# The output projection's first two tiles emitted inside attention, and head 7's first half ordered ahead of head 6's second half

## The chip, the cores and the metric

The kernel runs on one core of one Trainium2 chip. The metric is the device time of one execution in microseconds, as the median of several runs. Less is better. The engines are TensorE (PE; its weight loads are listed apart as PEld), VectorE (DVE), ScalarE (ACT), GpSimd (POOL) and SyncE (SP), which here issues the transfers.

## The reference

The kernel computes two layers of a decoder trunk over 1024 tokens of width 1024 in float32. Each layer normalises x, makes one wide input projection and feeds three branches: a causal convolution (256 channels), latent attention with 8 heads, and a spatial gating unit (256 channels). Each branch output is gated and RMS-normalised; the three are concatenated, go through one output projection and are added to x.

```python
for l in range(DEPTH):                       # 2
    h = _rms_norm(x, norm_g[l]); proj = h @ w_in[l]
    y_conv = _conv_branch(a, a_glu, ...) * silu(z_conv)
    y_mla  = _mla_branch(c_q, c_kv, k_rope, ...) * silu(z_mla)   # 8 heads, causal, 96 wide q/k, 64 wide v
    y_sg   = _sgu_branch(u_sg, v_sg, ...) * silu(z_sg)
    y = concatenate([rms(y_conv), rms(y_mla), rms(y_sg)])        # 256 + 512 + 256
    x = x + y @ w_out[l]
```

## The kernel before, in words

Tokens are cut into 8 tiles of 128. Every large product is made from operands split into a high and a low fp32r part, with three matmuls per product (`mm3`, L157): hi by hi, hi by lo, lo by hi. ScalarE casts the high part, VectorE subtracts it for the low part (`split`, L167 to L170). PSUM is given out as four single banks (`bank`, tag b1) and two double ones (`bank2`, tag b2). Scores, and the transposes of a whole token tile (`chan_of`, written pt or pty), use the double ones.

The order of the work is written out in two steps. `Flow` and, in attention, a planner hold estimated times and decide in which order instructions are emitted. The tile framework then fixes each engine's queue from that list by a clock of its own, so that work which is ready can pass work that isn't; on the chip each engine keeps that order. Memory is given out in pools that are opened and closed like a stack on two sides; a tile that takes over memory waits for whoever used it last.

Attention (`attention`, L982) keeps three lists: `sq` (transposes of q and k, scores with their softmax, weight splits and early loads), `tq` (transposes of probabilities for a head, a half of 512 queries and a key tile j) and `pq` (products with v, and `finish`, which transposes a pair of heads' sums, `ot`, and multiplies them into zsm). It takes the entry that can start first by its estimates. Half 0 has 4 key tiles, half 1 has 8. `tq` goes through the heads in order, half 0 before half 1. The scores of head h's half are emitted only after the previous head's last transpose of the same half, and the wide probabilities have four buffers (tag p1). The even heads' q and k lie in pool T1, the odd heads' in pool T. After head 7's half 0 is finished, tiles 0 and 1 of the attention output are normed (`early_norm`, L862): ScalarE squares, VectorE and GpSimd scale.

After attention pool T is closed and pool Ya opened in its place. For tiles 0 and 1 the branch outputs are transposed into yT (`chan_of`, written pty), which is a tile of Ya; the other tiles follow with two tiles' lead. `y_out` (L899) makes the projection of one token tile and one half of the output columns with 24 matmuls into the tile po, and `y_add` (L915) adds x and stores the result. The halves are c = 0 and 1, each over all 8 tiles. Loads of the side branches (`y_load`, tile yn) and of x (`x_load`, tile xr or xt) go through SP's queue. In the first layer the pass c = 1 also norms the next layer's input (`s0_next`, L954).

```python
        for i in (0, 1):                                      # L934
            sd, ym = early_src.pop(i)
            chan_of([...], y_tile(i, yp_), 0, f"pty{l}_{i}")
            y_load(i + 2); y_norm(i + 2); x_load(0, i)
    tq = []                                                   # L1136
    for h in range(H):
        for half in (0, 1):
            tq += [(h, half, j) for j in range(4 * half + 4)]
```

Of the kernel before, what the change touches and what calls it, by code (L numbers as in the profile page):

```python
# [126 lines left out]
def hybrid_trunk(ctx, tc, x, w, pc, pr, sgw, pww, cst, out):  # L127
# [235 lines left out]
    for l in range(L):  # L363
# [56 lines left out]
        def layer_norm_stats(srcs, mv, rstd):  # L420
# [5 lines left out]
            rsqrt(rstd, rstd)  # L426

        def v_done(p, o):
            vg = ap_.tile([P, 2, SW], F32, tag="e2k", bufs=5 - l, name=f"vg{l}_{p}")
            nc.scalar.activation(vg, pair(o), AF.Gelu_apprx_tanh)  # L430

            def rest():
                mv = ap_.tile([P, 2, 2], F32, tag="mv", bufs=4, name="mv")
                rstd = ap_.tile([P, 2], F32, tag="rstd", bufs=4, name="rstd")
                layer_norm_stats([vg[:, 0, :], vg[:, 1, :]], mv, rstd)
                for t in (0, 1):
                    nc.vector.tensor_scalar(vg[:, t, :], vg[:, t, :], mv[:, t, 0:1],
                                            rstd[:, t:t + 1], op0=ALU.subtract, op1=ALU.mult)
                flow.at(VN_LAG[l], gains)

            def gains():
                nc.gpsimd.tensor_tensor(out=vg, in0=vg, in1=bc_mid(slg, 2), op=ALU.mult)
                nc.gpsimd.tensor_tensor(out=vg, in0=vg, in1=bc_mid(slb, 2), op=ALU.add)
                if p % 2 == 0:
                    vn.append(sp.tile([P, NT // 2, SW], F32R, tag="h", bufs=5 - l, name=f"vl{l}_{p}"))
                hi, lo = vn[0][:, 2 * p:2 * p + 2, :], vn[-1][:, p % 2 * 2:p % 2 * 2 + 2, :]
                nc.scalar.copy(hi, vg)
                nc.gpsimd.tensor_tensor(out=lo, in0=vg, in1=hi.bitcast(F32), op=ALU.subtract)
            flow.at(0.8, rest)
# [78 lines left out]

        sgs = sp.tile([P, 2, SH, P], F32R, tag="h", bufs=5 - l, name=f"sgs{l}")
        nc.scalar.copy(sgs[:, 0], sgm)  # L530
# [79 lines left out]
        def conv_swish(p, nt):  # L610
            b = bank(f"cb{l}_{p}")
            for ct in (0, 1):
                for t in (0, 1):
                    tr(b[:, ct * 256 + t * P:ct * 256 + (t + 1) * P], nt[:, t, ct * P:(ct + 1) * P])
            sT = ap_.tile([P, 2, 256], F32, tag="sT", bufs=1, name="sT")
            th = ap_.tile([P, 2, 256], F32, tag="th", bufs=1, name="th")
            for ct in (0, 1):
                src = b[:, ct * 256:(ct + 1) * 256]
                nc.scalar.activation(th[:, ct, :], src, AF.Tanh, scale=dpc[:, 62 + ct:63 + ct],
                                     bias=dpc[:, 64 + ct:65 + ct])  # L620
                nc.scalar.activation(sT[:, ct, :], src, AF.Identity,
                                     scale=pcs[:, PC_LG + ct:PC_LG + ct + 1],
                                     bias=pcs[:, PC_LB + ct:PC_LB + ct + 1])
            nc.vector.scalar_tensor_tensor(out=sT, in0=th, scalar=1.0, in1=sT,
                                           op0=ALU.add, op1=ALU.mult)
            if not pws:
                pws.append(parts_of(pwt, "pws", nc.gpsimd))
            ss = parts_of(sT, f"ss{p}", nc.vector)
            flow.at(4.0, lambda: conv_point(p, ss))
# [3 lines left out]
        def parts_of(a, name, eng):  # L633
            t = sp.tile([P, 2, 2, 256], F32R, tag="h", bufs=5 - l, name=f"{name}_{l}")
            nc.scalar.copy(t[:, 0], a)
            eng.tensor_tensor(out=t[:, 1], in0=a, in1=t[:, 0].bitcast(F32), op=ALU.subtract)
            return t
# [36 lines left out]

        def latent(o, dst, c, half, gcol, first, acc):
            tk = slice(half * 512, (half + 1) * 512)
            split_gain(dst[:, 0, c, tk], dst[:, 1, c, tk], o, gcol)
            if first:
                nc.scalar.activation(acc, o, AF.Square)
            else:  # L680
                sq = cpool.tile([P, 512], F32, tag="sq", bufs=2, name="sq")
                nc.scalar.activation(sq, o, AF.Square)
                nc.gpsimd.tensor_tensor(out=acc, in0=acc, in1=sq, op=ALU.add)
# [9 lines left out]
        c2_cm, c2pool = open_pool(f"C2_{l}", "right")  # L693
        ckvT = c2pool.tile([P, 2, 2, S], F32R, name=f"ckvT{l}")

# [33 lines left out]
        for half in (0, 1):  # L729
            acc = c2pool.tile([P, 512], F32, tag="sqa", bufs=2, name="sqkv")  # L730
            for c in (0, 1):
                o = chan(un, c * P, half, half == 1 and c == 1, f"ckv{l}_{c}{half}")
                latent(o, ckvT, c, half, pcs[:, PC_KVN + c:PC_KVN + c + 1], c == 0, acc)
            flow.at(4.0, lambda half=half, acc=acc: mean_sq(0, half, acc, KVL))
        flow.at(8.0, kv_scales)
        sqq = None
        for u in range(3):
            un = Unit(l, f"CQ{u}")
            for half in (0, 1):
                for c in (0, 1):  # L740
# [4 lines left out]
                    cix = 2 * u + c  # L745
                    latent(o, cqT, cix, half, pcs[:, PC_QN + cix:PC_QN + cix + 1], cix == 0, sqq[half])
                if u == 2:
# [4 lines left out]


        q_cm, qp = open_pool(f"Q{l}", "left")
        ksb = qp.tile([P, NT, H, DQK], F32, name=f"ksb{l}")
        vsb = qp.tile([P, NT, MW], F32, name=f"vsb{l}")
        qsb = qp.tile([P, NT, H, DQK], F32, name=f"qsb{l}")

# [22 lines left out]
        for i in range(NT):  # L781
# [4 lines left out]
            for n, o in ((0, kps), (512, vps)):  # L786
                for k in (0, 1):
                    wh, wl = un.get(k)
                    mm3(o, (ckvT[:, 0, k, tk], ckvT[:, 1, k, tk]),
                        (wh[:, n:n + 512], wl[:, n:n + 512]), k == 0, k == 1)  # L790
# [5 lines left out]
        close_pool(c2_cm)  # L796
        t1_cm, t1p = open_pool(f"T1_{l}", "left")

        def query_out(u, i, o):
# [66 lines left out]
        def early_norm(i):  # L866
            ym = t1p.tile([P, 512], F32, tag=("p03", "os")[i], bufs=(1, 2)[i], name="yme")
            mla_norm(i, ym, t1p)
            early_src[i].append(ym)


        def open_t():
# [4 lines left out]
            return tp  # L877
        attention(nc, flow, t1p, open_t, late_splits, [lambda i=i: query(1, i) for i in range(2, NT)],
                  bank, bank2, mm, mm3, tr, split, split_gain, ident_b, mask_b,
                  ksb, qsb, vsb, zsm, dpc[:DQK, 66:67], (early_load, early_norm), l)  # L880
        close_pool(t_cm[0])
# [5 lines left out]
        ya_cm, yp_ = open_pool(f"Ya{l}", "right")  # L887
        yT, yns = {}, {}

# [33 lines left out]
        def x_load(c, i):  # L923
            if c == 1 and not last:

                xt = xts[i] = sp.tile([P, D], F32, tag="xt", bufs=2, name=f"xt{l + 1}_{i}")
                nc.sync.dma_start(xt[:, 0:512], xmid[i * P:(i + 1) * P, 0:512])
# [6 lines left out]
        for i in (0, 1):  # L934
            sd, ym = early_src.pop(i)
            blk = lambda t, k: t[:, k * P:(k + 1) * P]
            chan_of([blk(sd, 0), blk(sd, 1)] + [blk(ym, k) for k in range(4)] + [blk(sd, 2), blk(sd, 3)],
                    y_tile(i, yp_), 0, f"pty{l}_{i}")
            y_load(i + 2)
            y_norm(i + 2)  # L940
            x_load(0, i)
        y_load(4)
        close_pool(t1_cm)
# [10 lines left out]
        def s0_next(j):  # L954
            h = hs1[j] = sp.tile([P, D], F32, tag="h", bufs=4, name=f"h{l + 1}_{j}")
            s0_norm(l + 1, j, xts.pop(j), ng, sp, dst=h)
            if j < 4:
                flow.at(3.5, lambda: to_chan(h, nhT[0], j * P, f"pth{l + 1}_{j}"))

        hs1 = {}  # L960
        units = [Unit(l, "WO0"), Unit(l, "WO1")]
        for n, (c, i) in enumerate(seq):
# [8 lines left out]
            flow.step()  # L971
            y_out(units[c], c, i, i == NT - 1)
            if not last and c == 1:
# [3 lines left out]
        close_pool(ya_cm)  # L977
        if not last:
            hT, cs = nhT, ncs


def attention(nc, flow, t1p, open_t, late_splits, extra, bank, bank2, mm, mm3, tr, split, split_gain, ident_b, mask_b,  # L982
              ksb, qsb, vsb, zsm, kgain, early, l):
# [22 lines left out]
    def v_split(h):  # L1006
# [7 lines left out]
        est("dve", 0.6, est("act", 0.55, flow.t))  # L1014

    def qk_part(h, which, half):
        p_ = pool["t"] if h % 2 else t1p
        if h not in heads:
            heads[h] = [p_.tile([P, 2, S], F32R, tag=t, name=f"{t}{l}_{h}") for t in ("qT", "kT")]
        o = bank(f"qkt{l}_{h}{which}{half}")  # L1020
# [116 lines left out]
    for h in range(H):  # L1137
        for half in (0, 1):
            tq += [(h, half, j) for j in range(4 * half + 4)]
    pq = []  # L1140
    emitted = set()
# [40 lines left out]

    early_load, early_norm = early
    for i in (0, 1):
        sq.insert(len(sq) - NT + 1, ("load", i, 0))
    x_left = list(extra)
    while sq or tq or pq:
        cand = []
        if x_left:
            cand.append((flow.t, 3))  # L1190
# [5 lines left out]
        flow.t = max(flow.t, when)  # L1196
        if prio == 3:
            x_left.pop(0)()
            for e in busy:
                busy[e] = max(busy[e], flow.t - 1.0)  # L1200
            if not x_left:
                pool["t"] = open_t()
                v_split(0)
        elif prio == PRIO[0]:
# [18 lines left out]
        else:  # L1223
# [9 lines left out]
            else:  # L1233
                finish(h, half, *rest)
                if h == H - 1 and half == 0:
                    for i in (0, 1):
                        early_norm(i)
                        est("act", 0.6, flow.t)


# [77 lines left out]
```

## Time and profile before

| | us |
|---|---|
| median of 3 runs | 1284.22 (1283.05 to 1284.34) |
| profiled execution | 1283.21 |
| its span, first to last instruction | 1281.20 |
| TensorE busy | 1244.0 (97%) |
| TensorE weight loads busy | 1091.0 (85%) |
| VectorE busy | 797.0 (62%) |
| ScalarE busy | 531.7 (42%) |
| GpSimd busy | 397.9 (31%) |
| granted clock, mean | 0.993 of full speed |

The profile gives each instruction's start and length, and for idle time the instruction whose end released it. Weight loads run beside matmuls. Matmul ends are modelled, so that an idle time between matmuls looks shorter than the one between their weight loads. Names are those of the program's tiles: s scores, p probabilities, pt and pT their transposes, o the product with v, os and ot the sums of a pair of heads and their transposes, yme and yn the normed attention output, yse the side branches of tiles 0 and 1, pty and yT the transposed branch outputs, po the projection.

### The profile page before, as it was taken

Reading aid. Unit: us, or ns where it says so; the run is one execution under the profiler, and the core shown is the slowest. Engines: PE = TensorE matmul, PEld = TensorE weight load, DVE = VectorE, ACT = ScalarE, POOL = GpSimd, SP = SyncE. Lnnn points to the kernel's source line nnn. Section 1 sums busy time; section 2 is a strip of 40 time slices with the busy share of each in tenths; the row PEclk is TensorE's granted clock in tenths of the full one; section 3 lists DMA queues with packets and bytes.
Section 4 is the critical chain, followed back from the end, with each engine's and each line's share of the span. In section 5 each row is a group of like instructions: output and inputs, shape, how many; then the busy total and the mean of one; then the engine's idle time right before and its main releaser. Section 6 shows DMA issues by size and latency. Waiting matters only on the chain.

```text
span 1281.2 us, 19181 instructions
## 1 busy us (share of the span) xinstructions
PE 1244.0 (97%) x7502; PEld 1091.0 (85%) x7502; DVE 797.0 (62%) x1321; ACT 531.7 (42%) x1083; POOL 397.9 (31%) x388
## 2 busy tenths in 40 slices
PE   8999999999998999999999999999999989999998
PEld 7889999888996787878898999998889878777886
DVE  7589963114768888854454998621257788888431
ACT  6211243223436777730342122532243477786200
POOL 4822343544573000010147133444446700000000
PEclk9999999999998999999999999999999989999999
DMA  7121212212111000053432112111211100001333
GB/s 292 50 67 34 71 42 60 67 33 74 50 34 34 1 1 1 18 156 123 148 128 66 34 49 88 43 58 33 70 38 50 52 15 1 1 1 42 99 105 101
DMA packets 33818, 77.86 MB, mean 61 GB/s; under 512 B 3776, under 2 KB 12352, under 8 KB 33728
## 3 DMA queue, kind: packets, MB, share of 16 engines
q1 hardware_dynamic: 33728, 76.64, 19.1%
q8 instruction: 59, 0.97, 0.3%
q14 instruction: 31, 0.25, 0.1%
HBM read 64.05 MB, written 12.58 MB: 60 GB/s over the span
## 4 chain that ended last, share of the span: by engine, by line
PE 87%; DVE 5%; ACT 5%; issue 1%; POOL 1%; DMA 0%; SPq 0%; ACTq 0%; POOLq 0%; DVEq 0%
PE po L154 14%; PE cq L154 10%; PE s L154 8%; PE qps L154 7%; PE o L154 5%; PE pt L165 4%; PE ZC L154 4%; PE U L154 4%; PE ZS L154 4%; PE ZM L154 4%; PE ckv L154 3%; PE glu L154 3%; PE a L154 3%; PE pzk L154 3%; PE V L154 2%; PE kps L154 2%
## 5 line engine op out<-in xcount | busy, mean ns | idle before, releaser
L154 PE MATMUL po<-w,yT 128*128 128x512 f32 x768 | 184.7, 398 | 0.0
L213 POOL TENSOR_TENSOR w<-raw,w 128x1024 fp32r<-128x1024 f32 (+1 forms) x49 | 118.4, 2423 | 181.1 <-ACT w L210 113.5
L154 PEld LDWEIGHTS po<-w,yT 128*128 128x128 f32 x768 | 142.8, 188 | 33.1
L520 DVE SCALAR_TENSOR_TENSOR run<-yp,dpc,run 128x1024 f32<-128x1024 f32 x116 | 145.4, 1286 | 1.4
L154 PE MATMUL s<-kT,qT 96*128 96x384 f32 (+5 forms) x576 | 132.7, 359 | 3.5 <-ACT p L1059 3.4
L154 PE MATMUL o<-pT,vh 128*128 128x512 f32 (+3 forms) x384 | 128.8, 395 | 7.4 <-DVE pT L170 5.9
L154 PE MATMUL cq<-hT,w 128*128 128x512 f32 x576 | 132.0, 390 | 0.0
L154 PEld LDWEIGHTS cq<-hT,w 128*128 128x128 f32 x576 | 107.8, 188 | 22.2
L170 DVE TENSOR_TENSOR pT<-pt,pT 128x512 fp32r<-128x512 f32 x192 | 100.1, 549 | 18.7 <-ACT pT L169 18.1
L154 PEld LDWEIGHTS s<-kT,qT 96*128 96x128 f32 x576 | 96.4, 193 | 14.1 <-ACT p L1059 6.6
L165 PE MATMUL pt<-cst_sb,p 128*128 128x128 f32 x576 | 95.6, 280 | 10.3 <-DVE qT L170 10.3
L1059 ACT ACTIVATE p<-s,rs 128x128 f32<-128x128 f32 (+7 forms) x128 | 94.9, 742 | 24.6 <-DVE rs L1053 15.9
L1053 DVE TENSOR_REDUCE rs<-s 128x1 f32<-128x128 f32 (+7 forms) x128 | 95.8, 749 | 14.1 <-PE s L154 13.5
L169 ACT CAST pT<-pt 128x512 fp32r<-128x512 f32 x192 | 88.7, 481 | 35.0 <-PE pt L165 33.7
L1079 POOL TENSOR_TENSOR zsm<-zsm,rs 128x256 f32<-128x256 f32 x32 | 19.6, 612 | 266.4 <-DVE rs L1077 266.4
L154 PE MATMUL qps<-w,cqT 128*128 128x384 f32 x576 | 101.9, 337 | 0.0
L154 PEld LDWEIGHTS qps<-w,cqT 128*128 128x128 f32 x576 | 100.2, 188 | 0.3
L165 PEld LDWEIGHTS pt<-cst_sb,p 128*128 128x128 f32 x576 | 68.3, 143 | 21.6 <-DVE qT L170 8.6
L154 PEld LDWEIGHTS o<-pT,vh 128*128 128x128 f32 x384 | 65.4, 192 | 17.5 <-DVE pT L170 11.3
L174 DVE SCALAR_TENSOR_TENSOR cqT<-cq,pcs,cqT 128x512 fp32r<-128x512 f32 x24 | 18.0, 750 | 93.9 <-ACT cqT L173 93.9
L210 ACT CAST w<-raw 128x1024 fp32r<-128x1024 f32 (+1 forms) x47 | 49.6, 1057 | 59.5 <-PE a L154 15.0
L918 DVE TENSOR_TENSOR xr<-po,xr 128x512 f32<-128x512 f32 x24 | 16.6, 691 | 65.6 <-PE po L154 65.6
(319 smaller groups left out, 2270.8 us busy)
## 6 DMA issues: line engine op xcount, KB each, us to landing
raw<-in_w_dram SPq DMA_DIRECT2D x64, 512.0 KB, 3.5
raw<-in_w_dram SPq DMA_DIRECT2D x12, 576.0 KB, 3.7
xt<-in_x_dram SPq DMA_DIRECT2D x8, 512.0 KB, 8.4
xr<-xmid SPq DMA_DIRECT2D x16, 256.0 KB, 2.7
out_dram<-xr SPq DMA_DIRECT2D x16, 256.0 KB, 2.0
yn<-yside SPq DMA_DIRECT2D x24, 128.0 KB, 3.1
yside<-ug SPq DMA_DIRECT2D x8, 256.0 KB, 2.2
yside<-yc SPq DMA_DIRECT2D x8, 256.0 KB, 2.1
```

What stands on the lines that cost most here:

```text
L154: nc.tensor.matmul(o, lhsT=lhsT, rhs=rhs, start=start, stop=stop)
L165: nc.tensor.transpose(out=o, in_=in_, identity=ident[:k, :k])
L169: nc.scalar.copy(hi, src)
L170: nc.vector.tensor_tensor(out=lo, in0=src, in1=hi.bitcast(F32), op=ALU.subtract)
L174: nc.vector.scalar_tensor_tensor(out=lo, in0=src, scalar=gain, in1=hi.bitcast(F32), op0=ALU.mult, op1=ALU.subtract)
L210: nc.scalar.copy(wt[:, 0, :sz], raw[:, :sz])
L213: (eng or nc.gpsimd).tensor_tensor(out=wt[:, 1, :sz], in0=raw[:, :sz], in1=wt[:, 0, :sz].bitcast(F32), op=ALU.subtract)
L520: nc.vector.scalar_tensor_tensor(out=acc if j == TAPS - 1 else run, in0=yp[:, j:j + S], scalar=wc, in1=run, op0=ALU.mult, op1=ALU.add)
L918: nc.vector.tensor_tensor(out=xr, in0=o, in1=xr, op=ALU.add)
L1053: nc.vector.tensor_reduce(out=sm[:, 1, t:t + 1], in_=src if nb > 1 else o[:, :wd], axis=AX.XY if nb > 1 else AX.X, op=ALU.max, negate=True)
L1059: nc.scalar.activation(pr_[:, :n].rearrange("p (b n) -> p b n", b=nb), src, AF.Exp, bias=sm[:, 1, t:t + 1], accum_out=sm[:, 0, t:t + 1])
L1079: nc.gpsimd.tensor_tensor(out=z, in0=z, in1=sm[:, 2, :].unsqueeze(2).broadcast_to([P, 4, DV]), op=ALU.mult)
```

## The change

Five things change together.

1. A pool E of two tiles (tags qT and kT, 8 KB a partition each) is opened in the first layer and stays to the end. The even heads' q and k lie there instead of in T1; qsb moves to T1. In the second layer the same two tiles also take v's split parts, the gating and pointwise weights, the latent kv operand; the next layer's normed input goes there in pairs.
2. yT of tiles 0 and 1 lies in these tiles, and their transposes and their 48 matmuls for c = 0 (`early_chan`, `early_out`) are a list `filler` in attention's planner. An entry is emitted when it is due and nothing else can start; what is left is emitted at the end.
3. The last 20 entries of `tq` are reordered: head 7's half 0 (4 entries) goes ahead of head 6's half 1 (8 entries).
4. Head 1's q and k are the first tiles of pool T, ahead of v's.
5. After attention, tiles 0 and 1 need only `y_add`; xt moves from pool S to Ya, and S keeps two h buffers in the second layer instead of four.

```diff
+        HB = 2 if l else 5
...
-                if p % 2 == 0:
-                    vn.append(sp.tile([P, NT // 2, SW], F32R, tag="h", bufs=5 - l, name=f"vl{l}_{p}"))
+                if p % 2 == 0 and l == 0:
+                    vn.append(sp.tile([P, NT // 2, SW], F32R, tag="h", bufs=HB, name=f"vl{l}_{p}"))
+                elif p == 0:
+                    keep["v"] = ep.tile([P, NT, SW], F32R, tag="qT", name=f"vl{l}")
+                    vn.append(keep["v"][:, :NT // 2, :])
...
+            both = ep.tile([P, 2, 2 * SH * P], F32R, tag="kT", name=f"sgpw{l}")
...
+        ckvT = [ep.tile([P, 2, S], F32R, tag=t, name=f"ckvT{l}_{t}") if l else
+                c2pool.tile([P, 2, S], F32R, name=f"ckvT{l}_{t}") for t in ("qT", "kT")]
...
+        if l == 0:
+            e_cm, ep = open_pool("E", "left")
...
-        qsb = qp.tile([P, NT, H, DQK], F32, name=f"qsb{l}")
+        qsb = t1p.tile([P, NT, H, DQK], F32, name=f"qsb{l}")
...
+        def early_chan(i):
+            sd, ym = early_src.pop(i)
+            yT[i] = ep.tile([P, 2, KC, P], F32R, tag=("qT", "kT")[i], name=f"yT{l}_{i}")
+            chan_of([...], yT[i], 0, f"pty{l}_{i}")
+        wo = [Unit(l, "WO0"), Unit(l, "WO1")]
+        def early_out(i, k):
+            if i not in early_po:
+                early_po[i] = bank2(f"po{l}_0_{i}")[:, :512]
+            mm3(early_po[i], (yT[i][:, 0, k, :], yT[i][:, 1, k, :]), wo[0].get(k), k == 0, k == KC - 1)
...
-                xt = xts[i] = sp.tile([P, D], F32, tag="xt", bufs=2, name=f"xt{l + 1}_{i}")
+                xt = xts[i] = yp_.tile([P, D], F32, tag="xt", bufs=2, name=f"xt{l + 1}_{i}")
...
         for i in (0, 1):
-            chan_of([...], y_tile(i, yp_), 0, f"pty{l}_{i}")
             y_load(i + 2)
             y_norm(i + 2)
             x_load(0, i)
+            y_add(early_po[i], 0, i)
...
-            h = hs1[j] = sp.tile([P, D], F32, tag="h", bufs=4, name=f"h{l + 1}_{j}")
+            if j % 2 == 0:
+                hpairs.append(ep.tile([P, 2, D], F32, tag=("qT", "kT")[j // 2 % 2], name=f"h{l + 1}_{j}"))
+            h = hs1[j] = hpairs[-1][:, j % 2, :]
...
-            y_out(units[c], c, i, i == NT - 1)
+            if c or i not in early_po:
+                y_out(wo[c], c, i, i == NT - 1)
...
+    cut = len(tq) - 20
+    tq[cut:] = tq[cut + 8:cut + 12] + tq[cut:cut + 8] + tq[cut + 12:]
...
+        if filler:
+            cand.append((max(filler[0][0], flow.t), 4))
...
+        if prio == 4:
+            filler.pop(0)[1]()
...
             if not x_left:
                 pool["t"] = open_t()
+                operands(1)
                 v_split(0)
...
                     for i in (0, 1):
                         early_norm(i)
                         est("act", 0.6, flow.t)
+                    filler += [(flow.t + 3.0, lambda: early_chan(0)), (flow.t + 4.0, lambda: early_chan(1))]
+                    filler += [(flow.t + 6.5, lambda i=i, k=k: early_out(i, k)) for i in (0, 1) for k in range(KC)]
+    for _, fn in filler:
+        fn()
```

## Rows read from the trace of the kernel before

**Rows 1.** The page, busy us of each engine, share of the span and instructions.
```profile
PE 1244.0 (97%) x7502; PEld 1091.0 (85%) x7502; DVE 797.0 (62%) x1321; ACT 531.7 (42%) x1083; POOL 397.9 (31%) x388
```

**Rows 2.** Windows: stretch, us, busy of PE, PEld, DVE, ACT, POOL; granted clock; DMA.
```profile
535.00:551.20 16.20, 13.50 (x90) 10.73 (x90) 11.94 (x25) 10.73 (x25) 1.72 (x3) 1.00 0.04 11
551.20:565.00 13.80, 13.80 (x71) 11.30 (x70) 9.56 (x16) 5.76 (x13) 2.71 (x5) 1.00 0.62 185
1166.00:1182.10 16.10, 13.39 (x90) 10.65 (x89) 11.86 (x24) 10.65 (x25) 1.72 (x3) 1.00 0.19 52
```

**Rows 3.** Waits of weight loads, 535:551.2: waiter <- releaser: us, times, longest.
```profile
PEld ot L165 <- DVE os L1108: 1.5, 1, 1.5
PEld o L154 <- ACT pT L169: 1.0, 2, 0.9
PEld pty L165 <- DVE yme L858: 0.7, 2, 0.4
PEld o L154 <- DVE pT L170: 0.7, 2, 0.4
PEld pty L165 <- ACT p L1059: 0.5, 1, 0.5
PEld pt L165 <- DVE pT L170: 0.2, 1, 0.2
```

**Rows 4.** Timeline of TensorE, end of the first layer's attention: start, us, instruction.
```profile
530.36 0.60 PE L165 MATMUL pt<-cst_sb,p 128*128 128x128 f32 x4
...
535.22 0.60 PE L165 MATMUL pt<-cst_sb,p 128*128 128x128 f32 x4
...
538.97 0.66 PE L165 MATMUL pt<-cst_sb,p 128*128 128x128 f32 x4
...
546.36 0.44 PE L154 MATMUL o<-pT,vh 128*128 128x384 f32 x1 [0.52 <-ACT pT L169]
...
549.09 0.31 PE L154 MATMUL o<-pT,vh 128*128 128x128 f32 x1
550.79 0.65 PE L165 MATMUL ot<-cst_sb,os 128*128 128x128 f32 x4 [1.40 <-DVE os L1108]
```

**Rows 5.** Timeline of ScalarE, same stretch.
```profile
524.91 0.69 ACT L1059 ACTIVATE p<-s,rs 128x512 f32<-128x512 f32 x1
...
530.73 1.12 ACT L1059 ACTIVATE p<-s,rs 128x1024 f32<-128x1024 f32 x1
...
536.34 0.80 ACT L1059 ACTIVATE p<-s,rs 128x640 f32<-128x640 f32 x1
...
544.61 0.63 ACT L854 ACTIVATE yme<-zsm 128x512 f32<-128x512 f32 x1 [0.65 <-DVE zsm L1117]
```

**Rows 6.** One merged piece of the chain (start, us), then groups by line.
```profile
578.25 5.60 PE po L154 x24
...
L170 DVE TENSOR_TENSOR yT<-pty,yT 128x1024 fp32r<-128x1024 f32 x16 | 19.6, 1224 | 18.7 <-ACT yT L169 18.7
...
L918 DVE TENSOR_TENSOR xr<-po,xr 128x512 f32<-128x512 f32 x24 | 16.6, 691 | 65.6 <-PE po L154 65.6
...
L169 ACT CAST yT<-pty 128x1024 fp32r<-128x1024 f32 x16 | 16.2, 1012 | 48.4 <-PE pty L165 48.3
```

**Rows 7.** SP's queue at attention's end; issue to landing of xr.
```profile
550.28 0.42 SPq L931 DMA_DIRECT2D xr<-in_x_dram  x1
...
xr<-in_x_dram SPq DMA_DIRECT2D x8, 256.0 KB, 2.8
```

**Rows 8.** Timeline at the layer boundary; then a piece of the chain.
```profile
649.88 0.42 SPq L452 DMA_DIRECT2D rows<-in_pr_dram  x1
...
653.79 1.28 DVE L304 SCALAR_TENSOR_TENSOR h<-xt,s0st,ng 128x1024 f32<-128x1024 f32 x1 [0.73 <-POOL s0st L178]
...
656.89 4.75 POOL L213 TENSOR_TENSOR w<-raw,w 128x1024 fp32r<-128x1024 f32 x2
...
676.27 5.47 PE glu L154 x24
```

More of the change, by code (lines that the diff above doesn't have):

```diff
@@ L426, in layer_norm_stats @@
             rsqrt(rstd, rstd)
+        HB = 2 if l else 5
+        keep = {}
         def v_done(p, o):
@@ L443, in gains @@
                 nc.gpsimd.tensor_tensor(out=vg, in0=vg, in1=bc_mid(slb, 2), op=ALU.add)
-                if p % 2 == 0:
-                    vn.append(sp.tile([P, NT // 2, SW], F32R, tag="h", bufs=5 - l, name=f"vl{l}_{p}"))
+                if p % 2 == 0 and l == 0:
[3 more added lines that the diff above has]
+                    vn.append(keep["v"][:, :NT // 2, :])
+                elif p == 2:
+                    vn.append(keep["v"][:, NT // 2:, :])
                 hi, lo = vn[0][:, 2 * p:2 * p + 2, :], vn[-1][:, p % 2 * 2:p % 2 * 2 + 2, :]
@@ L527, in hybrid_trunk @@
                                 compare_op=ALU.is_ge, fill=0.0, base=0, channel_multiplier=-1)
-        sgs = sp.tile([P, 2, SH, P], F32R, tag="h", bufs=5 - l, name=f"sgs{l}")
+        if l == 0:
+            sgs = sp.tile([P, 2, SH, P], F32R, tag="h", bufs=HB, name=f"sgs{l}")
+        else:
+            both = ep.tile([P, 2, 2 * SH * P], F32R, tag="kT", name=f"sgpw{l}")
+            sgs = both[:, 0].rearrange("p (a g t) -> p a g t", a=2, g=SH)
+            keep["pw"] = both[:, 1].rearrange("p (a c n) -> p a c n", a=2, c=2)
         nc.scalar.copy(sgs[:, 0], sgm)
@@ L626, in conv_swish @@
             if not pws:
-                pws.append(parts_of(pwt, "pws", nc.gpsimd))
+                pws.append(parts_of(pwt, "pw", nc.gpsimd))
             ss = parts_of(sT, f"ss{p}", nc.vector)
@@ L633, in parts_of @@
         def parts_of(a, name, eng):
-            t = sp.tile([P, 2, 2, 256], F32R, tag="h", bufs=5 - l, name=f"{name}_{l}")
+            t = keep.pop(name, None)
+            if t is None:
+                t = sp.tile([P, 2, 2, 256], F32R, tag="h", bufs=HB, name=f"{name}_{l}")
             nc.scalar.copy(t[:, 0], a)
@@ L673, in hybrid_trunk, with latent @@
         ms = cp.tile([P, 2, NT], F32, tag="ms", name=f"ms{l}")
-        def latent(o, dst, c, half, gcol, first, acc):
+        def latent(o, dst, half, gcol, first, acc):
             tk = slice(half * 512, (half + 1) * 512)
-            split_gain(dst[:, 0, c, tk], dst[:, 1, c, tk], o, gcol)
+            split_gain(dst[:, 0, tk], dst[:, 1, tk], o, gcol)
             if first:
@@ L693, in hybrid_trunk @@
         c2_cm, c2pool = open_pool(f"C2_{l}", "right")
-        ckvT = c2pool.tile([P, 2, 2, S], F32R, name=f"ckvT{l}")
+        ckvT = [ep.tile([P, 2, S], F32R, tag=t, name=f"ckvT{l}_{t}") if l else
+                c2pool.tile([P, 2, S], F32R, name=f"ckvT{l}_{t}") for t in ("qT", "kT")]
         tabs = [cpool.tile([P, NT, ROPE], F32, name=f"tab{n}_{l}") for n in (0, 1)]
@@ L732, in hybrid_trunk @@
                 o = chan(un, c * P, half, half == 1 and c == 1, f"ckv{l}_{c}{half}")
-                latent(o, ckvT, c, half, pcs[:, PC_KVN + c:PC_KVN + c + 1], c == 0, acc)
+                latent(o, ckvT[c], half, pcs[:, PC_KVN + c:PC_KVN + c + 1], c == 0, acc)
             flow.at(4.0, lambda half=half, acc=acc: mean_sq(0, half, acc, KVL))
@@ L745, in hybrid_trunk @@
                     cix = 2 * u + c
-                    latent(o, cqT, cix, half, pcs[:, PC_QN + cix:PC_QN + cix + 1], cix == 0, sqq[half])
+                    latent(o, cqT[:, :, cix, :], half, pcs[:, PC_QN + cix:PC_QN + cix + 1], cix == 0, sqq[half])
                 if u == 2:
@@ L751, in hybrid_trunk @@
         close_pool(h0_cm)
+        if l == 0:
+            e_cm, ep = open_pool("E", "left")
         q_cm, qp = open_pool(f"Q{l}", "left")
@@ L788, in hybrid_trunk @@
                     wh, wl = un.get(k)
-                    mm3(o, (ckvT[:, 0, k, tk], ckvT[:, 1, k, tk]),
+                    mm3(o, (ckvT[k][:, 0, tk], ckvT[k][:, 1, tk]),
                         (wh[:, n:n + 512], wl[:, n:n + 512]), k == 0, k == 1)
@@ L869, in early_norm @@
             early_src[i].append(ym)
+        blk = lambda t, k: t[:, k * P:(k + 1) * P]
+        yT, early_po = {}, {}
+        def early_chan(i):
+            sd, ym = early_src.pop(i)
+            yT[i] = ep.tile([P, 2, KC, P], F32R, tag=("qT", "kT")[i], name=f"yT{l}_{i}")
+            chan_of([blk(sd, 0), blk(sd, 1)] + [blk(ym, k) for k in range(4)] + [blk(sd, 2), blk(sd, 3)],
+                    yT[i], 0, f"pty{l}_{i}")
+        wo = [Unit(l, "WO0"), Unit(l, "WO1")]
[3 more added lines that the diff above has]
+            mm3(early_po[i], (yT[i][:, 0, k, :], yT[i][:, 1, k, :]), wo[0].get(k), k == 0, k == KC - 1)
         def open_t():
@@ L877, in open_t @@
             return tp
-        attention(nc, flow, t1p, open_t, late_splits, [lambda i=i: query(1, i) for i in range(2, NT)],
+        attention(nc, flow, t1p, ep, open_t, late_splits, [lambda i=i: query(1, i) for i in range(2, NT)],
                   bank, bank2, mm, mm3, tr, split, split_gain, ident_b, mask_b,
-                  ksb, qsb, vsb, zsm, dpc[:DQK, 66:67], (early_load, early_norm), l)
+                  ksb, qsb, vsb, zsm, dpc[:DQK, 66:67], (early_load, early_norm, early_chan, early_out), l)
         close_pool(t_cm[0])
@@ L887, in hybrid_trunk @@
         ya_cm, yp_ = open_pool(f"Ya{l}", "right")
-        yT, yns = {}, {}
+        yns = {}
         def y_load(i):
@@ L934, in hybrid_trunk @@
         for i in (0, 1):
[L935 to L938, printed above, removed]
             y_load(i + 2)
@@ L958, in s0_next @@
                 flow.at(3.5, lambda: to_chan(h, nhT[0], j * P, f"pth{l + 1}_{j}"))
-        hs1 = {}
-        units = [Unit(l, "WO0"), Unit(l, "WO1")]
+        hs1, hpairs = {}, []
         for n, (c, i) in enumerate(seq):
@@ L977, in hybrid_trunk, with attention @@
         close_pool(ya_cm)
-        if not last:
+        if last:
+            close_pool(e_cm)
+        else:
             hT, cs = nhT, ncs
-def attention(nc, flow, t1p, open_t, late_splits, extra, bank, bank2, mm, mm3, tr, split, split_gain, ident_b, mask_b,
+def attention(nc, flow, t1p, ep, open_t, late_splits, extra, bank, bank2, mm, mm3, tr, split, split_gain, ident_b, mask_b,
               ksb, qsb, vsb, zsm, kgain, early, l):
@@ L1014, in v_split, with operands @@
         est("dve", 0.6, est("act", 0.55, flow.t))
+    def operands(h):
+        p_ = pool["t"] if h % 2 else ep
+        heads[h] = [p_.tile([P, 2, S], F32R, tag=t, name=f"{t}{l}_{h}") for t in ("qT", "kT")]
     def qk_part(h, which, half):
-        p_ = pool["t"] if h % 2 else t1p
         if h not in heads:
-            heads[h] = [p_.tile([P, 2, S], F32R, tag=t, name=f"{t}{l}_{h}") for t in ("qT", "kT")]
+            operands(h)
         o = bank(f"qkt{l}_{h}{which}{half}")
@@ L1181, in p_when @@
         return pq[0][0] + SL_P if pq else None
-    early_load, early_norm = early
+    early_load, early_norm, early_chan, early_out = early
+    filler = []
     for i in (0, 1):
@@ L1196, in attention @@
         flow.t = max(flow.t, when)
-        if prio == 3:
+        if prio == 4:
+            filler.pop(0)[1]()
+        elif prio == 3:
             x_left.pop(0)()
```

## The prediction

> **What bounds the kernel now.** I read the page's busy times first. TensorE is busy 1244.0 of 1281.2 us, 97% [rows 1]; no other engine comes near, so a change here is worth what TensorE idles less, plus or minus what it makes TensorE wait. Second, the stretches around each attention's end. From 535.00 to 551.20, the last part of the first layer's attention, TensorE is busy 13.50 of 16.20 us; in the 13.80 us behind it, where the output projection starts, it is busy throughout, and the second layer's attention ends like the first (13.39 of 16.10) [rows 2]. The granted clock is 1.00 in all three, so there is no clock to be won. Third, what ended the idle time in that stretch, counted on the weight loads, because matmul ends are modelled and reach into the gap behind them: 1.5 us before the last transposes of the attention output (ot), 1.0 before products whose hi part ScalarE was still casting, 0.7 before the transposes of the normed tile (yme), 0.7 and 0.2 behind VectorE's lo parts, 0.5 behind a softmax: 4.6 us [rows 3].
> The Trainium skill (Perfetto Trace Analysis, Identifying the Most-Contended Engine) says that matmul occupancy is no good measure of the headroom and that the weight loads' busy time is to be read instead. The trace bears that out here: the matmul row of the stretch shows 2.7 us idle, the weight loads' waits 4.6. By the former the change could give at most 5.4 us in two layers, by the latter 9.2.
>
> Where the 4.6 us come from is seen in the order of work [rows 4, 5]. Head 7's first half is transposed from 535.22, its second half from 538.97, and the last product starts at 549.09; then nothing is left to issue until VectorE has added the halves, and ot comes at 550.79 after 1.40 us. In the middle, ScalarE squares two normed tiles from 544.61 (0.63 us, and a second one behind it), in front of casts that the products wait for; the product at 546.36 stood 0.52 us.
>
> **The change, part by part.** Per layer:
>
> 1. *The filler.* Two tiles' first output half, 2 x 24 matmuls, 24 of which take 5.60 us [rows 6], so 11.2 us, can now be issued before attention is over. Nothing is removed: the work moves into gaps. Before, it could not start there, since its operand yT lay in a pool that opens only after attention; now yT lies in the tiles of the even heads' q and k, free once head 6's scores are done. The gap before ot (1.5) is covered wholly: at most 3.1 of the 11.2 us (4.6 less 1.5) fit into the gaps ahead of it, so some 8 us stand ready. I count 1.5.
>
> 2. *Head 7's first half ahead of head 6's second half.* Its softmax ends at 525.60 (524.91 + 0.69) [rows 5], so its transposes can start then and not at 535.22: 9.6 us earlier. The squares and the norm move with it, from 544.61 to about 535, and both yT can be written by about 540. So the waits that the norm makes in the last stretch, 0.7 for yme and 0.9 of the 1.0 for the cast behind the squares, go from there: 1.6. The squares then stand in front of casts of head 6; I take 0.3 for that (bounds 0 and 0.9, the cast wait of before), so 1.3 is kept.
>
> 3. *The other gaps* of the stretch (0.7 + 0.2 + 0.5, with 0.1 left of the cast waits: 1.5) are short waits between a transpose and its product. TensorE takes its queue in order, and the queue's order is fixed by the build's own clock, so a filler stands in a gap only where that clock saw one. Bounds 0 and 1.5; I take a third, 0.5, since these are gaps of 0.5 us and less [rows 3], such as a queue meets on the chip without having been planned for them.
>
> 4. *What head 7's first half covered.* Its transposes and products stood between the last scores' softmax and the first transpose of the second half (535.22 to 538.97, 3.75 us). Head 7's second-half probabilities take the buffers that head 6's second half gives back: the softmax of tile 7 starts at 530.73, as the fifth group of transposes is issued (530.36), and that of tile 4 ends at 537.14 [rows 4, 5]. This chain of 6.4 us now follows head 6's second half directly, with less beside it. What can stand there are the 16 pty transposes, 0.1 us each (four from 550.79, the next matmul at 551.20 [rows 2, 4]), 1.6 us. Bounds 0 and 3.0 (a bank's hold, below); I take 1.0.
>
> 5. *PSUM.* The fillers' transposes and sums use the two double banks, which scores use too. Both early sums hold one until they are added, and the add needs xr, whose memory came free only with the last product (SP issues it at 550.28, the last product ends at 549.40; landing 2.8 us [rows 4, 7]). From the last product's end: 0.9 to the issue, 2.8 landing, 0.69 add, 0.8 for tile 2's eight transposes, 1.01 cast, 1.22 lo [rows 6]: tile 2's projection can start 6.2 us after it with the hi part alone, 7.4 us with both. The filler left over (8 us) and ot (0.4) cover that, so I count 0; without them it would be an idle of up to 7. Placing head 1's q and k first in its pool gives yn memory that is free earlier; it can only shorten this, and I count 0.
>
> 6. *Memory moved in the second layer and at the layer boundary* (v, sgs, pw, ckvT, h pairs in the two tiles; two h buffers instead of four; xt in Ya; qsb in T1). Each tile is taken long after its earlier user is done, except one: the rows load at 649.88 may now lie where xt was and wait for the last norm (653.79 + 1.28 = 655.07), 5.2 us. Behind it in SP's queue stand weight loads, behind these POOL's weight split, which ends at 661.64; TensorE needs it at 676.27 [rows 8]. 14.6 us of cover hide it: 0. Without cover it would be 5.2 once.
>
> Sum per layer: 1.5 + 1.3 + 0.5 - 1.0 = 2.3; two layers 4.6. The second layer's projection and the first's run without idle to the next stage, so the end moves by as much. The profiled execution took 1283.21 (span 1281.20, 2.01 around it), so 1278.6; the median of the runs shown is 1.01 higher, 1284.22, which gives **1279.6**. By the bounds a layer gives from 1.5 + 0.7 + 0 - 3.0 = -0.8 to 4.6.
>
> **The rivals.**
>
> *Everything fills* (A): the queue puts po matmuls into all gaps, 4.6 per layer: 1284.22 - 9.2 = 1275.0. For it: a po matmul, once its yT and its bank are there, waits for nothing else. Against: the fillers come only from about 540, and part of the waits lies ahead of that (the stretch begins at 535 [rows 2, 3]).
>
> *One bank held* (B), no change: the transposes of early tile 0 get a double bank before the last scores. It is held for 0.8 + 1.01 + 1.22 = 3.0 us [rows 6], and one score and its softmax wait so long, with TensorE empty, since po needs the same banks. 3.3 - 3.0 = 0.3 per layer: 1283.6. For it: in the run of before pty takes a bank as soon as one is free, and the planner doesn't count that bank. The filler coming late, with only ot's gap filled and the join costing its middle, ends there too.
>
> *Both held* (C), slower: tiles 0 and 1 each take a bank before the last two scores, so the softmax chain that sets head 7's second half starts 6.0 us late. 3.3 - 6.0 = -2.7 per layer: 1289.6. It decides from 3.3 us of delay; from 4.6 it is slower by more than 0.2%. For it: both are due 3 to 4 us after head 7's first half is finished, about when head 6's last transposes go out. Against: the planner issues a filler only when nothing else is ready, and scores come first at equal times.
>
> *The change doesn't do what it says*: the build's order puts all 48 matmuls behind attention. Then the filler still covers ot's gap, which is in the 2.3; this ends in the forecast's lower half or in B.
>
> **How the numbers follow.** Forecast 0.48, A 0.10, B 0.24, C 0.18. About 0.2% (2.57 us) is what a measurement of this kernel can tell from no change: faster is below 1281.65, so forecast and A, 0.58; same is B, 0.24; slower is C, 0.18. The forecast's own range is 1276.0 to 1281.6. The range that should hold 8 in 10 reaches from just below A (1274.5) across B to 1287.0 and leaves out most of C.
>
> **What would show it.** Right: po matmuls of tiles 0 and 1 start near 540 to 545 and stand among pt and o; the wait of ot for os is gone or short; yme's squares come near 535; no idle from ot to tile 2's projection. The join shows as a wait of pt for a softmax before head 7's second half. Wrong: s or p waiting for a double bank behind pty (B, C); the last product more than 3 us later than 549.09; idle of TensorE between po of tile 1 and tile 2; or the stretch from 650 to 680 longer, which would be the memory edits.

## The result: slower by 1.3%, and the profile after

The changed kernel takes 1301.70 us (median of 4 runs, 1297.36 to 1303.28) against 1284.18 for the kernel before (4 runs): ratio 1.0134, 95% interval 1.0123 to 1.0146. The forecast was 1279.6, its range ended at 1287.0, and slower had a chance of 0.18. The prediction was wrong, in sign and in size.

The profiled execution took 1303.28 us with a span of 1301.6, that is 20.4 more than before. Nothing new is to be done: TensorE has the same 7502 instructions, 8.2 us more busy time (at a lower clock one instruction is longer) and 12 us more idle time [rows 1]. The page's busy times:

```profile
PE 1252.2 (96%) x7502; PEld 1099.1 (84%) x7502; DVE 800.9 (62%) x1321; ACT 533.0 (41%) x1083; POOL 398.4 (31%) x388
```

Where it went is found by taking the same work in both traces. The second layer's first 24 glu products start at 688.17 in the chain of after, at 676.27 in that of before [rows 8]: 11.9 us. Of these 1.0 comes in the first 40 us (granted clock 0.91 there, before 0.96; the first glu products at 42.37 instead of 41.35); the run with TensorE kept busy, below, has the changed memory too and shows 0.96, so the change doesn't bring it by itself. The other 10.9 arise between 535 and 580, and the remaining 8.5 of the 20.4 come in the second layer, whose attention ends with the same waits but the one for the second residual (1188 to 1212). Windows of after (us, busy of PE, PEld, DVE, ACT, POOL; granted clock; DMA), to be read against [rows 2]; the second line is a part of the first:

```profile
535.00:551.20 16.20, 13.04 (x66) 10.06 (x66) 9.26 (x16) 8.84 (x19) 1.73 (x3) 0.89 0.01 1
548.00:550.00 2.00, 2.00 (x6) 1.60 (x5) 0.00 (x0) 0.00 (x0) 0.00 (x0) 0.50 0.00 0
551.20:566.00 14.80, 14.53 (x79) 11.98 (x77) 4.55 (x8) 4.09 (x9) 0.00 (x0) 1.00 0.00 1
566.00:577.40 11.40, 6.21 (x25) 5.19 (x26) 6.85 (x13) 5.62 (x13) 2.20 (x4) 0.70 0.66 200
577.40:600.00 22.60, 22.60 (x116) 18.68 (x115) 9.84 (x13) 4.74 (x7) 1.10 (x2) 1.00 0.52 169
```

Two stretches are bad: the one from 535, with 66 matmuls where 90 stood and a granted clock down to 0.50 in its part, and the one from 566, in which TensorE is busy 6.2 of 11.4 us at a granted clock of 0.70. TensorE's timeline there (start, us, instruction, in brackets the idle time ahead and its releaser), to be held against [rows 4]:

```profile
536.40 0.38 PE L165 MATMUL pty<-cst_sb,yse 128*128 128x128 f32 x2
...
537.66 1.31 PE L154 MATMUL s<-kT,qT 96*128 96x384 f32 x6
...
539.79 0.65 PE L165 MATMUL pty<-cst_sb,yme 128*128 128x128 f32 x4 [0.19 <-DVE yme L877]
...
542.66 1.14 PE L154 MATMUL s<-kT,qT 96*128 96x320 f32 x6
...
543.71 0.39 PE L165 MATMUL pty<-cst_sb,yse 128*128 128x128 f32 x2
...
546.64 4.61 PE L154 MATMUL po<-w,yT 128*128 128x512 f32 x12 [1.89 <-ACT p L1100]
551.08 1.47 PE L165 MATMUL pt<-cst_sb,p 128*128 128x128 f32 x12
552.31 4.38 PE L154 MATMUL po<-w,yT 128*128 128x512 f32 x18
...
563.07 0.63 PE L154 MATMUL po<-w,yT 128*128 128x512 f32 x2
...
564.47 1.25 PE L154 MATMUL o<-pT,vh 128*128 128x384 f32 x6
567.12 0.66 PE L165 MATMUL ot<-cst_sb,os 128*128 128x128 f32 x4 [1.40 <-DVE os L1149]
570.79 1.97 PE L165 MATMUL pty<-cst_sb,yn 128*128 128x128 f32 x8 [3.02 <-DVE yst L874]
573.82 1.97 PE L165 MATMUL pty<-cst_sb,yn 128*128 128x128 f32 x8 [1.05 <-DVE xr L954]
```

Read from the top: tile 0's transposes (pty, 536.40) take one of the two double banks and hold it until VectorE has written the lo part of yT (542.17 + 1.21 = 543.38). The last two scores therefore go through the other one, in turn: that of query tile 5 at 537.66, that of query tile 4 only when tile 5's softmax has been read (541.61 + 0.91 = 542.52), at 542.66. Tile 1's transposes then take the first bank (543.71), and po finds none for its sum until the last softmax is read: the 1.89 us ahead of 546.64, behind which the clock falls. That softmax is also what the second half's transposes (pt, 551.08) need; it ends at 546.50, where [rows 5] end at 537.14. ScalarE and VectorE there:

```profile
541.61 0.91 ACT L1100 ACTIVATE p<-s,rs 128x768 f32<-128x768 f32 x1
542.17 1.21 DVE L170 TENSOR_TENSOR yT<-pty,yT 128x1024 fp32r<-128x1024 f32 x1
545.70 0.80 ACT L1100 ACTIVATE p<-s,rs 128x640 f32<-128x640 f32 x1
```

The last two of the 48 po matmuls are issued at 563.07, ahead of the last nine products. So nothing of the filler is left when ot waits its 1.40 us and when the transposes of tile 2 wait behind it. The waits of the weight loads, first in 535:566, then in 566:584 (against [rows 3]):

```profile
PEld po L154 <- ACT p L1100: 2.1, 1, 2.1
PEld o L154 <- DVE pT L170: 1.6, 3, 0.7
PEld pty L165 <- DVE yme L877: 0.4, 1, 0.4
PEld o L154 <- ACT pT L169: 0.3, 1, 0.3
...
PEld pty L165 <- DVE yst L874: 3.3, 1, 3.3
PEld ot L165 <- DVE os L1149: 1.5, 1, 1.5
PEld pty L165 <- DVE xr L954: 1.5, 1, 1.5
```

The list names VectorE's yst as the releaser of the first pty; but VectorE's own timeline has the addition of tile 0's residual ending at 570.73 (570.05 + 0.68), just ahead of 570.79; the run with the sums given back early, below, tests this. The second wait is the same bank question for tile 1, and the chain of waits shows what it hangs on, the residual's transfer of 5.02 us:

```profile
567.55 0.43 SPq L869
...
568.03 5.02 DMA xr<-in_x_dram
...
573.07 0.70 DVE xr L954
...
573.82 1.97 PE pty L165 x8
```

### The profile page after: what moved, and what is told of

Same layout as the page of the kernel before. It is cut to its first block, busy times and chain, and to the rows that moved or that the text cites. A ratio compares the mean times of both kernels' runs of the same rounds, so it can differ in the third digit from the quotient of the medians.

```text
span 1301.6 us, 19180 instructions
## 1 busy us (share of the span) xinstructions
PE 1252.2 (96%) x7502; PEld 1099.1 (84%) x7502; DVE 800.9 (62%) x1321; ACT 533.0 (41%) x1083; POOL 398.4 (31%) x388
## 4 chain that ended last, share of the span: by engine, by line
PE 87%; ACT 5%; DVE 5%; POOL 1%; issue 1%; DMA 1%; SPq 0%; ACTq 0%; POOLq 0%; DVEq 0%
PE po L154 14%; PE cq L154 10%; PE s L154 8%; PE qps L154 7%; PE o L154 5%; PE pt L165 4%; PE ZC L154 4%; PE U L154 4%; PE ZS L154 4%; PE ZM L154 3%; PE ckv L154 3%; PE glu L154 3%; PE a L154 3%; PE V L154 3%; PE pzk L154 3%; PE kps L154 2%
## 5 line engine op out<-in xcount | busy, mean ns | idle before, releaser
L154 PE MATMUL po<-w,yT 128*128 128x512 f32 x768 | 188.5, 403 | 3.8 <-ACT p L1100 3.8
L154 PEld LDWEIGHTS po<-w,yT 128*128 128x128 f32 x768 | 146.1, 192 | 37.8 <-ACT p L1100 4.3
```

Of the source, the lines that this page charges most:

```text
L154: nc.tensor.matmul(o, lhsT=lhsT, rhs=rhs, start=start, stop=stop)
```

## The experiments

Ratios are to the kernel before, run on the same chip, with 95% intervals. Two parts of the loss were suspected: **ahead** of the last product (the bank taken before the last scores, the late softmax) and **behind** it (no filler left, while the next transposes wait for banks and the clock falls).

**Without the new order.** The reordering line is taken out of the changed kernel; everything else stays, the memory moves too.

```
-    tq[cut:] = tq[cut + 8:cut + 12] + tq[cut:cut + 8] + tq[cut + 12:]
```

> The changed kernel with the old order of head 6's and head 7's halves. TensorE's queue then has pty and po behind head 7's last transposes, as before the change, so most of the 11.2 us of po still stand behind the last product. Theory M (the filler was spent before the last product, so that the latency behind it lies bare, and the clock falls there): the loss goes, 1279 to 1284. Rival memory (the tiles moved into pool E, fewer h buffers): most of the loss stays, over 1293. Rival bank (an early tile holds a double bank before the last score): the loss goes too, since pty is behind all scores; M and bank are told apart by the next two runs.

1281.63 us (10 runs), ratio 0.9983 (0.9974 to 0.9993). Here the filler falls due late and stands behind the last product of attention (550.40), ahead of ot (557.73). The memory edits cost nothing that can be measured, and the loss needs the early filler.

**The order alone**, in the kernel before.

```
+    cut = len(tq) - 20
+    tq[cut:] = tq[cut + 8:cut + 12] + tq[cut:cut + 8] + tq[cut + 12:]
```

> The kernel before with nothing but the new order of the two halves. Theory M: the order by itself costs little, 1281 to 1287 (the join of head 6's and head 7's second halves against the norm moved out of the last stretch). Rival order (the join is the harm): 1293 or more.

1280.90 us (10 runs), ratio 0.9979 (0.9969 to 0.9988): not the cause either, and a gain of 2.5 us by itself. Its waits in 536:564 are 3.1 us where [rows 3] have 4.6; the casts that stood behind the squares are gone from the list:

```profile
PEld ot L165 <- DVE os L1108: 1.5, 1, 1.5
PEld o L154 <- DVE pT L170: 0.6, 2, 0.3
PEld pty L165 <- ACT p L1059: 0.4, 1, 0.4
PEld pty L165 <- DVE yme L858: 0.4, 1, 0.4
PEld L154 <- issue: 0.2, 1, 0.2
```

**Filler only after the last score.**

```
-        if filler:
+        if filler and not sq:
```

> The changed kernel, but a filler is emitted only when all scores are. No pty takes a double bank ahead of a score any more; po still stands among head 7's last transposes and is used up before the last product. Bank alone: 1281 to 1286. Theory M: the part before the last product (some 3 us a layer) goes, the part behind it (5.5 us of waits and some 3 us of half clock a layer) stays: 1294 to 1298.

1291.77 us (4 runs), ratio 1.0061 (1.0046 to 1.0076), a little under the theory's range: the part ahead is worth 9.9 us in two layers, more than I had put on it. The last product ends at 560.05 instead of 565.72. But all 48 po are issued before it here too, and of the part behind only the wait for the second residual is nearly gone (0.2 us where 1.5 stood):

```profile
559.48 0.57 PE L154 MATMUL o<-pT,vh 128*128 128x256 f32 x4
561.45 0.66 PE L165 MATMUL ot<-cst_sb,os 128*128 128x128 f32 x4 [1.40 <-DVE os L1149]
565.29 3.77 PE L165 MATMUL pty<-cst_sb,yn 128*128 128x128 f32 x16 [3.19 <-DVE yst L874]
568.71 4.68 PE L154 MATMUL po<-w,yT 128*128 128x512 f32 x16
```

**The same bank, single.** The early transposes take two single banks each, nothing else is changed; all 48 products remain filler.

```
-                    yT[i], 0, f"pty{l}_{i}")
+                    yT[i], 0, f"pty{l}_{i}", 2)
```

> The changed kernel with the two hoisted sets of transposes in two single PSUM banks each instead of one double bank; the 48 products still stand among the last head's transposes, and both sums still hold the double banks. Theory (the early transposes take a double bank ahead of the last two scores and delay the last softmax): the scores are on time, 1290 to 1294 us, near the run with filler only after the scores. Rival (the products among the transposes cost it, the bank does not): 1299 to 1303 us.

1292.39 us (4 runs), ratio 1.0072 (1.0058 to 1.0085), as the theory said. The last softmax ends at 540.89, 5.6 us earlier, and the last product at 560.26, 5.5 earlier, although po matmuls still stand among the last head's transposes. The part ahead is therefore the double banks that the two sets of early transposes take, not the filler's place among the last head's transposes:

```profile
540.10 0.79 ACT L1100 ACTIVATE p<-s,rs 128x640 f32<-128x640 f32 x1
```

**Tile 1 behind attention.** Only tile 0 is filler; tile 1 is transposed and projected behind attention, as in the kernel before.

```
-  filler += [(flow.t + 3.0, lambda: early_chan(0)), (flow.t + 4.0, lambda: early_chan(1))]
-  filler += [... for i in (0, 1) for k in range(KC)]
+  filler += [(flow.t + 3.0, lambda: early_chan(0))]
+  filler += [... for k in range(KC)]
...
```

> The changed kernel, but tile 1 is transposed and projected behind attention, into a tile of pool Ya, as before the change; only tile 0 is filler. The bank is still held before the last score, the 5.6 us of tile 1 cover what comes behind the last product. Theory M: the part behind goes, 1283 to 1288, with the wait of ot and of pty<-yn short and the clock at 1.00 there. Bank alone: 1298 to 1302.

1285.31 us (10 runs, 1283.44 to 1290.84), ratio 1.0018 (1.0006 to 1.0030), inside the theory's range. Tile 1's 24 products cover what lies behind ot: po goes on from 560.12, after 0.5 us for yT, with the clock at 1.00. The wait of ot itself was to become short and did not (1.5 us), since tile 0's products are spent ahead of it here too. Ahead of the last product the score of tile 4 is as late as in the profile after (542.46 here), but po starts at 544.09, not at 546.64: no transposes of tile 1 stand in the bank that its sum takes.

```profile
544.09 6.67 PE L154 MATMUL po<-w,yT 128*128 128x512 f32 x24
...
559.20 0.66 PE L165 MATMUL ot<-cst_sb,os 128*128 128x128 f32 x4 [1.39 <-DVE os L1154]
560.12 4.01 PE L154 MATMUL po<-w,yT 128*128 128x512 f32 x16 [0.26 <-ACT yT L169]
```

**Both cuts.** The edits of "Filler only after the last score" and "Tile 1 behind attention" together.

> Both cuts at once: filler only after the last score product, and tile 1 transposed and projected behind attention, so 24 products are filler and 24 follow the last product. Theory (the loss has two parts, filler ahead of the last scores and nothing left behind the last product): both parts are gone and the covered waits are left as a gain, 1277 to 1281 us. Rival (tile 1 behind attention or the join of the two orders has a price of its own, which is what keeps the earlier tile-1 run above before): 1284 us or more.

1283.29 us (11 runs), ratio 0.9999 (0.9990 to 1.0008): a miss, between the two ranges. The bank and the cover behind ot are right, but the 24 products of tile 0 are again spent early, from 541.98 on. ot waits its 1.5 us, the first po of tiles 0 and 1 wait 0.7 and 0.5 for yT: 4.0 us of waits at the first attention's end, where the run with the order alone has 3.1. In the second layer the clock falls as well, to 0.57 in 1186:1190.

The two parts of the loss don't simply add. Holding the filler back until the last score takes 9.9 us off when both tiles are filler (1301.70 to 1291.77), but 2.0 when only tile 0 is (1285.31 to 1283.29). So most of the part ahead needs tile 1's early transposes as well.

**The sums given back early.** The run with filler only after the last score, with the residual tiles of rows 0 and 1 loaded and added inside attention.

```
+  filler.insert(1, (flow.t + 3.0, lambda: early_x(0)))
+  filler.insert(3, (flow.t + 4.0, lambda: early_x(1)))
+  filler.insert(4 + KC, (flow.t + 6.5, lambda: early_add(0)))
+  filler.append((flow.t + 6.5, lambda: early_add(1)))
...
-            y_add(early_po[i], 0, i)
```

> Filler only after the scores, and the residual tiles of rows 0 and 1 loaded, and their sums added, inside attention, so that the two double banks are free before the last product. Theory (behind the last product the next transposes wait for a bank, which the addition gives back only after its residual tile has landed): they start some 2.2 us earlier per layer and the clock falls for less time, 1283 to 1288 us. Rival (they wait for the norm of tile 2 anyway): 1290 to 1292 us.

1284.55 us (10 runs), ratio 1.0009 (1.0000 to 1.0019): 7.2 us less than without it. The waits behind the last product (560:580) name no addition and no yst any more:

```profile
PEld ot L165 <- DVE os L1149: 1.5, 1, 1.5
PEld pty L165 <- DMA yn<-yside: 1.5, 3, 1.0
PEld pty L165 <- DVE yn L877: 0.7, 1, 0.7
PEld po L154 <- ACT yT L169: 0.3, 1, 0.3
```

So tile 2's transposes did wait for a bank, and the bank for the addition behind the residual's transfer.

**TensorE kept busy in the wait.** Again the run with filler only after the last score, with 14 products in front of tile 2's transposes whose sum nobody reads.

```
+        warm_o = bank(f"keep{l}")
+        for k in range(14):
+            mm(warm_o, yT[0][:, 0, k % KC, :], wo[0].get(k % KC)[0], True, True)
```

> Filler only after the scores, and 14 products whose result nobody reads behind the last output transposes, so that TensorE is busy in the 3.2 us in which it waits for the transposes of tile 2. Theory (half the clock from 563 to 570 us costs some 2.4 us a layer by itself): 1286 to 1289 us. Rival (the clock's fall costs nothing beside the wait): 1291 to 1293 us.

1287.10 us (5 runs), ratio 1.0031 (1.0019 to 1.0044): more work, and 4.7 us less time. The windows in the first layer without the extra products, then with them (columns as above):

```profile
562.00:564.00 2.00, 0.11 (x1) 0.00 (x0) 1.80 (x4) 0.13 (x2) 0.84 (x2) 0.86 0.81 238
564.00:570.00 6.00, 4.71 (x19) 4.29 (x20) 3.85 (x7) 3.15 (x6) 0.84 (x2) 0.50 0.68 235
```

```profile
562.00:564.00 2.00, 2.00 (x10) 1.65 (x9) 1.97 (x4) 0.73 (x2) 0.00 (x0) 1.00 0.83 258
564.00:570.00 6.00, 4.90 (x31) 3.96 (x30) 4.18 (x8) 3.27 (x6) 1.10 (x2) 1.00 0.71 230
```

The wait itself is as long as it was (pty 3.7 us behind the start of ot, 560.58 to 564.30, against 3.8); what is saved is the clock, 1.00 instead of 0.50 from 564 to 570. By the medians that is 2.3 us a layer, but not all of it is these products': of the 5.2 us between the two profiled spans (1290.0 and 1284.8) 0.9 stand in the first 40 us and 0.9 around 1030:1040, where the granted clock was 0.91 and 0.66 without them, 0.96 and 0.83 with them. At the two places themselves 1.3 and 2.2 us are saved.

**A version that might beat both.** The transposes only after the last score; the po matmuls emitted only when attention has no transposes or products left, and their sums in single banks, whose turn comes only behind the last head's transposes.

```
-        if filler:
+        if filler and (len(filler) > 2 * KC and not sq or not tq and all(e[1] != "pv" for e in pq)):
...
-                early_po[i] = bank2(f"po{l}_0_{i}")[:, :512]
+                early_po[i] = bank(f"po{l}_0_{i}")
```

> Both tiles' transposes only after the last score, and their sums in two of the single banks, taken after the last head's transposes, so that no product of theirs can be issued before the last few of attention; 24 then stand around the last products and 24 behind ot. Theory (the filler is worth something only where TensorE has nothing else, ahead of ot and behind it): the run with the order alone less the wait for os, 1.4 us in each layer, 1277 to 1280 us. Rival (the early sums or the single banks have a price that eats this, as in the run with both cuts): 1281 us or more.

1280.42 us (11 runs), ratio 0.9977 (0.9968 to 0.9986). It lies between the two ranges, and level with the order alone (0.9979). Tile 0's 24 products now stand around the last products and cover most of ot's gap, 24 follow ot, nothing is idle for long. Yet the waits in 538:566 sum to 3.7 us, against 3.1 with the order alone:

```profile
PEld o L154 <- DVE pT L170: 1.8, 3, 0.7
PEld ot L165 <- DVE os L1149: 0.6, 1, 0.6
PEld po L154 <- ACT yT L169: 0.5, 1, 0.5
PEld pty L165 <- ACT p L1100: 0.4, 1, 0.4
PEld pty L165 <- DVE yme L877: 0.4, 1, 0.4
```

ot gained 0.9, the products lost 1.2 to VectorE's lo parts: the two yT now written inside attention cost VectorE 1.2 us each [rows 6] just where TensorE waits for its pT. That the yT writes are what delays pT was read from the order of the engines' work, not tested by itself.

## Why the prediction was wrong

**Step 1 failed, and with it the cover that step 5 took from it**: "at most 3.1 of the 11.2 us (4.6 less 1.5) fit into the gaps ahead of it, so some 8 us stand ready", and "The filler left over (8 us) and ot (0.4) cover that, so I count 0". None stood ready: the filler doesn't only fill gaps of the trace before. It is issued as soon as its operands are there by the build's clock, in front of work that is ready a little later, and in the traces TensorE keeps that order. All 48 matmuls were spent ahead of the last product. That does no harm there (the run with filler only after the scores ends its last product at 560.05; 549.40 of before plus 11.2 of moved work is 560.6), but it uncovers what lay behind. Step 5 priced just that: "without them it would be an idle of up to 7". From the run without the new order, where the filler stands behind attention, to the one with filler only after the scores, the difference is 10.1 us, 5.1 a layer: up to 2.3 by the clock and, from the early additions, 3.6 by the banks, which overlap.

**The bank hold (rivals B and C)** was the second half, 9.9 us in two layers by the runs with filler after the scores and without, 9.3 by the one with single banks. B had the mechanism, tile 0's transposes taking a double bank ahead of the last scores, but its hold was mis-sized: 0.8 + 1.01 + 1.22 = 3.0 us. Measured, it runs from 536.40 to 543.38: 7.0. The sum left out that the middle four transposes wait for the norm (yme, 539.79), and that ScalarE and VectorE have other work queued ahead. So one bank, held past both last scores, which then shared the other, was enough to make the last softmax 5.6 us late, close to the 6.0 that C needed two banks for. But the late softmax alone is not the price: with only tile 0 as filler it was as late, and the hold cost 2.0 us in two layers, not 9.9. Most of the rest came with the bank of tile 1, which C had, though here it was taken behind the last score and stopped po, not a score: 2.1 us of waiting in each layer, and behind it 12 po in 4.4 us (546.64 to 551.08) at a granted clock of 0.66 (546:551), where 24 take 5.60 [rows 6]. What else adds to the 9.9 was not taken apart. And neither rival asked what a late softmax does to the filler, nor added the uncovered tail: C's 1289.6 holds one part of the loss, not both.

**Step 5's transfer** was short too: 2.8 us from issue to landing [rows 7], 5.02 for the second residual in the first layer. The loads of tiles 2 to 4 are issued around it, and the DMA engines are 0.94 busy in 568:570; that these loads delay it was not tested.

**"there is no clock to be won"** was true of the windows, and left out that one can be lost. The profile after shows 0.50 in 548:550, behind po's wait for a bank, and 0.50 in 571:577, where TensorE had been idle since 565.7 but for ot's four transposes. The Trainium skill (TensorE: Matmul & The Clock Gate, The HAM clock gate) says that an array that has been idle falls to half its clock and stays there until it has been busy again; the trace agrees (1.00 down to 0.50, 2.4 to 1.2 GHz, back at 1.00 from 578), and eight transposes took 1.97 us at 0.50, where they take 1.04 at 1.00 (both in the runs above, at 570.79 here and at 573.23 in the run with filler only after the scores).

**Right were** the size of step 2, and step 6. The order alone took the cast waits away and left 3.1 of 4.6 us, 1.5 a layer, where 1.3 was kept; two layers give 3.0, and 2.5 were measured. Step 4's join (1.0 lost) didn't show: in that run none but transposes of tile 0's branch outputs wait for a softmax, 0.4. What step 2 said of yT failed, though: "both yT can be written by about 540"; in the profile after tile 0's ends at 543.38 and tile 1's at 547.06. The memory edits cost nothing at the layer boundary: 11.9 us is the lag of the glu products and 11.92 that of the 48 po before it (650.24 against 638.32). Step 3's gain of 0.5 did not come; in the last version of the experiments those short waits grew.

## What to carry to other kernels

Filler covers a wait only if something keeps it back until then: a planner that issues it when its operands are there spends it early, so ask of each covered wait what holds the filler for it (here, a bank whose turn comes late). Before hoisting transposes, count the buffers that they share with the chain that is critical, and size the hold from the first write to the last read, with the waits of every operand in between. And when idle time opens behind a moved block, add what the clock loses in it.

## What the runs showed of the hardware that was not expected

Work that computes nothing can pay: 14 products more per layer, 3.3 us of TensorE, made the kernel 4.7 us faster (1291.77 to 1287.10), because the granted clock stayed at 1.00 instead of falling to 0.50; of the 5.2 us between the two profiled executions 3.5 arise at these two places. And covering waits and removing them did not add: filler behind attention in the old order, the new order without filler, and the new order with filler around the last products came out at 0.9983, 0.9979 and 0.9977, with intervals that overlap. The cheapest of the three, two added lines, is the one to keep.
